# Unsplit weights and operands in a full float32 product: the mixers' output projections and the mixed output projection

## The chip, the cores and the metric

The kernel runs on one core of one Trainium2 chip. The metric is the device time of one execution in microseconds (us). TensorE (PE) multiplies, VectorE (DVE) and ScalarE (ACT) do elementwise work, GpSimd (POOL) issues the gathers and SyncE (SP) the loads of weights.

## The reference, cut to what matters

Two blocks run one after the other on 256 tokens of width 1024. The first has two layers of a hybrid mixer and a gated feed-forward part. The change lies in the two mixers:

```python
def hybrid_mixer(h, w_in, ret_out, ..., ssd_out, w_o):
    u = h @ w_in
    q, k, v, g_ret, z, xbc, dt, gate_ret, gate_ssd = split(u)
    yr = silu(g_ret) * rmsnorm(retention(rotary(q), rotary(k), v))     # 256 x 2048
    o_ret = yr @ ret_out                                               # 2048 -> 1024
    ys = rmsnorm_by_group(ssd(conv(xbc), dt) * silu(z)) * ssd_norm_w   # 256 x 2048
    o_ssd = ys @ ssd_out                                               # 2048 -> 1024
    merged = sigmoid(gate_ret) * o_ret + sigmoid(gate_ssd) * o_ssd
    return merged @ w_o                                                # 1024 -> 1024
```

`x = x + hybrid_mixer(rmsnorm(x))`, then the feed-forward part. The second block (attention, Fourier and pooling branches, and a layer of experts picked by keys) comes before and after: its work on the context runs first, and the gathering of its experts for the context goes on as background work under both mixers.

## The kernel before

Activations lie with features on the partitions: a tile is 128 features by 256 tokens, eight of them (NB) make the width. Weights come in units of 128 x 1024 float32 (512 KB): eight blocks of 128 x 128 for one column block of the output. `Stream` (class at line 232) works through a list of steps, one or two units each. It keeps four loads in flight (`stage`, four buffers, line 328, on SP's queue) and splits up to three units ahead (`split`, three buffers): `split_one` writes a high half in the rounded type fp32r on ACT (line 304) and the remainder, the low half, on DVE (line 305). A step marked `raw` gets the unit as it was loaded, without a split; the Fourier and pooling constants and the expert keys already run so.

A product of split weights and split operand is three matmuls (`mm3`, lines 448 to 450): high x high, high x low, low x high. `proj` does this for the eight blocks of a unit, `pairs` for a row of units, two units to one PSUM tile, with an `evac` that takes each pair out of PSUM. The operands are split too: `halves` (lines 455, 456, or 458, 459 with a scale) writes the high half on ACT and the low half on DVE. Two such operands exist, x2 and y2; layer 0 reads the residual from y2 and collects the mixers' outputs in x2, layer 1 the other way round.

In `mixer` the steps of a layer stand in this order, with 213 units in all: q and k of heads 0 to 2 and v and gate of heads 0 and 1; a flush; **ret0** (8 units: first half of ret_out); the other heads, z and x of group 0; **ret1** (8); groups 1 and 2; **ssd0** (8: first half of ssd_out); group 3 and the first gate; a flush; **ssd1** (8); the second gate (gs, 8); **wo** (8); then the feed-forward part. The operand of ret0 and ret1 comes from `finish` of each head (line 735, then halves), that of ssd0 and ssd1 from `six` of each group (line 882, then halves), that of wo from the evac of the second gate (line 915, then halves with scale). Chains of small steps (a head's scores and values, a group's scan) are set some steps after their projections (`later`), and lie between the matmuls of whatever runs then: group 0's chain in ret1, group 2's in ssd0.

The background (`peer_jobs`) is a list of jobs that each step releases by a credit: a slot of 1.75 steps gathers 1 MB of expert rows on POOL's queue, takes a dot product on DVE (line 1476) and adds the row to an accumulator on DVE (line 1487); jobs of routing sort keys on DVE. Each background instruction is held behind the latest split (`queue`, `st.last`). The order on each engine within these bounds is the scheduler's.

Of the kernel before, what the change touches and what calls it, by code (L numbers as in the profile page):

```python
# [10 lines left out]
F32 = mybir.dt.float32  # L11
F32R = mybir.dt.float32r
# [218 lines left out]

class Stream:
# [121 lines left out]
def tile_model(ctx: ExitStack, tc: tile.TileContext, a: dict, out: bass.AP):  # L354
# [28 lines left out]
    x2 = keep.tile([128, 2, NB, T], F32R, name="x2")  # L383
    y2 = keep.tile([128, 2, NB, T], F32R, name="y2")
    xh, xl, yh, yl = x2[:, 0], x2[:, 1], y2[:, 0], y2[:, 1]
# [185 lines left out]
    def pairs(arr, i0, n, evac, m=x2, kb=NB, k0=0, wide=False):  # L571
# [13 lines left out]
        for b in range(2 if wide else 0, n):  # L585
            def go(w, b=b):
                if b % 2 == 0:
                    held[0] = mm(2, T)
                proj(held[0][:, b % 2], w, m, k0, kb)
                if b % 2 or b == n - 1:  # L590
                    evac(b // 2, held[0])
            st.w(go, (arr, i0 + b), width=kb * 128)
# [16 lines left out]
    sides = ((y2, x2), (x2, y2))  # L609

    def mixer(l):
        W = a[f"first{l}"]
        o_ret, o_ssd = arena(ORET, NB, T), arena(OSSD, NB, T)
        x2, y2 = sides[l]
        xh, xl, yh, yl = x2[:, 0], x2[:, 1], y2[:, 0], y2[:, 1]
# [73 lines left out]
        def head_vg(h):  # L689
# [42 lines left out]
            def finish():  # L732
                p = stat(T)
                spread(y[1], p)
                V.scalar_tensor_tensor(fin, fin, 0.5, bc(p[:, None, :], [128, 4, T]), op0=OP.mult, op1=OP.mult)
                b = 4 * (h % 2)
                halves(yh[:, b:b + 4], yl[:, b:b + 4], fin)
# [12 lines left out]
        def ret_half(kh, i0):  # L750
# [6 lines left out]
            pairs(W, i0, 8, evac, y2)  # L757
# [18 lines left out]
        def group_x(g, i0):  # L776
# [101 lines left out]
            def six():  # L878
                p = stat(T)
                spread(y[1], p)  # L880
                for b in range(4):
# [18 lines left out]
        def ssd_half(kh, i0):  # L900
# [6 lines left out]
            pairs(W, i0, 8, evac, y2)  # L907

        def gate_ssd(i0):
            def evac(i, p):  # L910
# [5 lines left out]
                halves(yh[:, s], yl[:, s], t, 0.5)  # L916
# [16 lines left out]
        head_qk(0)  # L933
        st.w(dt_step, (W, FIRST_AT["dt"]), width=256)
# [592 lines left out]
    def peer_dense(l, filler=None, rate=0.0, between=None, middle=None):  # L1527
# [7 lines left out]
        wh, wl = [[w[:, i] for i in range(3)] for w in (yh, yl)]  # L1535
# [83 lines left out]
        def prep(i):  # L1619
# [4 lines left out]
            halves(wh[i % 3], wl[i % 3], f)  # L1624
# [194 lines left out]
```

## Time and profile before

| what | value |
|---|---|
| time, median of 3 runs | 4349.99 us (4347.65 to 4356.72) |
| the profiled execution: time, span | 4350.16 us, 4348.4 us |
| PE busy, matmul records | 4016.6 us (92%), 31186 |
| DVE busy | 3483.3 us (80%) |
| ACT busy | 2206.7 us (51%) |
| mean granted clock of PE | 0.964 |
| splits on DVE (line 305) | 1243, 1500.8 us |
| the two mixers without feed-forward | 344 to 982 us and 1204 to 1763 us of the span |

PE's busy share counts pipelined records that overlap, so 92% is not 92% of what PE can do; the distance between starts tells more. Shares over the whole span hide the stages: DVE is busy 90% or more in most of the slices from 430 to 2000 us, where the mixers and the background run together.

### The profile page before, as it was taken

To read this page: it belongs to the slowest core of one execution; us is meant where nothing else is said; L and a number is where in the kernel's file an instruction comes from. 1 tells how busy PE (TensorE), PEld (TensorE's weight loads), DVE (VectorE), ACT (ScalarE), POOL (GpSimd) and SP (SyncE) were. 2 spreads that over 40 slices of the span, in tenths; PEclk is the share of its full clock that TensorE was granted. 3 is DMA by queue.
4 is the path that set the end of the run, shared out by engine and by line. 5 is a ranking of instruction groups with operands and counts; after the bars stand their busy time and mean duration, and the time that the engine had idled before them with its cause. 6 is when DMAs were issued, how large, how long until landed. Compare 5 with 4: busy or idle time off the path is not lost.

```text
span 4348.4 us, 78619 instructions
## 1 busy us (share of the span) xinstructions
PE 4016.6 (92%) x31186; PEld 3804.5 (87%) x31186; DVE 3483.3 (80%) x6710; ACT 2206.7 (51%) x3473; POOL 393.0 (9%) x260
## 2 busy tenths in 40 slices
PE   8998888899999888998988899999999989899999
PEld 6887877789999888997878889999988988899999
DVE  5678999999989999998899986665575799855555
ACT  5655545554545555445744445555445444444444
POOL 0001111122222112221100000000000000000000
PEclk9998999999999999999999999999999999999999
DMA  6666765688878777886764588776644445776665
GB/s 210 213 209 239 251 234 202 249 321 317 315 286 335 257 261 292 315 331 234 257 219 155 170 281 258 241 239 215 186 139 135 152 144 179 260 231 206 206 187 151
DMA packets 293314, 1008.77 MB, mean 232 GB/s; under 512 B 25745, under 2 KB 92945, under 8 KB 255185
## 3 DMA queue, kind: packets, MB, share of 16 engines
q1 hardware_dynamic: 250608, 698.32, 49.5%
q0 software_dynamic: 36864, 268.45, 16.3%
q10 hardware_dynamic: 5472, 36.97, 2.1%
q8 instruction: 245, 4.01, 0.4%
q14 instruction: 125, 1.02, 0.1%
HBM read 966.94 MB, written 36.70 MB: 231 GB/s over the span
## 4 chain that ended last, share of the span: by engine, by line
PE 56%; DVE 33%; issue 5%; ACT 3%; DMA 3%; SPq 0%; DVEq 0%; ACTq 0%
PE mm L450 11%; PE mm L448 10%; PE mm L449 10%; DVE w L305 9%; PE ot L448 4%; PE ot L450 4%; PE ot L449 4%; DVE rows L1476 3%; DVE acc L1487 3%; DVE arena L1566 2%; ACT w L304 2%; PE st L449 1%; PE st L450 1%; PE st L448 1%; DMA rows<-gates 1%
## 5 line engine op out<-in xcount | busy, mean ns | idle before, releaser
L305 DVE TENSOR_TENSOR w<-stage,w 128x1024 fp32r<-128x1024 f32 (+1 forms) x1243 | 1500.8, 1213 | 571.8 <-ACT w L304 566.6
L304 ACT ACTIVATE w<-stage 128x1024 fp32r<-128x1024 f32 (+1 forms) x1243 | 1301.0, 1051 | 940.6 <-PE mm L450 474.7
L450 PE MATMUL mm<-x,w 128*128 128x256 f32 x4896 | 1402.4, 287 | 64.9 <-DVE w L305 64.2
L448 PE MATMUL mm<-x,w 128*128 128x256 f32 x4896 | 1409.8, 288 | 37.5 <-ACT x L458 10.8
L449 PE MATMUL mm<-x,w 128*128 128x256 f32 x4896 | 1398.0, 286 | 2.8 <-DVE x L459 1.8
L450 PEld LDWEIGHTS mm<-x,w 128*128 128x128 f32 x4896 | 940.3, 192 | 82.4 <-DVE w L305 79.7
L448 PEld LDWEIGHTS mm<-x,w 128*128 128x128 f32 x4896 | 942.5, 193 | 57.4 <-ACT w L304 13.7
L449 PEld LDWEIGHTS mm<-x,w 128*128 128x128 f32 x4896 | 941.5, 193 | 11.6 <-issue 5.0
L450 PE MATMUL mm<-y,w 128*128 128x256 f32 x1776 | 517.6, 293 | 47.8 <-DVE w L305 47.0
L1470 POOL DMA_INDIRECT rows<-in_table,idx x256 | 392.8, 1534 | 1843.0 <-DVE acc L1487 1219.5
L448 PE MATMUL mm<-y,w 128*128 128x256 f32 x1776 | 520.3, 293 | 28.1 <-ACT w L304 12.3
L449 PE MATMUL mm<-y,w 128*128 128x256 f32 x1776 | 512.7, 289 | 1.6 <-DVE y L456 0.9
L450 PE MATMUL ot<-y,w 128*128 128x256 f32 (+1 forms) x1616 | 454.7, 282 | 3.3 <-DVE w L305 3.3
L448 PE MATMUL ot<-y,w 128*128 128x256 f32 (+1 forms) x1616 | 454.7, 282 | 1.5 <-DVE arena L1131 1.5
L449 PE MATMUL ot<-y,w 128*128 128x256 f32 (+1 forms) x1616 | 454.1, 281 | 1.2 <-DVE y L456 1.2
L450 PEld LDWEIGHTS mm<-y,w 128*128 128x128 f32 x1776 | 347.7, 196 | 59.3 <-DVE w L305 57.8
L448 PEld LDWEIGHTS mm<-y,w 128*128 128x128 f32 x1776 | 349.0, 197 | 35.5 <-ACT w L304 14.4
L449 PEld LDWEIGHTS mm<-y,w 128*128 128x128 f32 x1776 | 348.8, 197 | 5.2 <-issue 2.9
L1487 DVE SCALAR_TENSOR_TENSOR acc<-rows,dots,acc 128x1024 f32<-128x1024 f32 x254 | 324.2, 1276 | 0.0
L1476 DVE SCALAR_TENSOR_TENSOR rows<-rows,h 128x1024 f32<-128x1024 f32 x256 | 311.1, 1215 | 7.3 <-DMA rows<-in_table,idx 7.2
L448 PEld LDWEIGHTS ot<-y,w 128*128 128x128 f32 (+1 forms) x1616 | 302.1, 187 | 6.8 <-DVE arena L1131 2.2
L450 PEld LDWEIGHTS ot<-y,w 128*128 128x128 f32 (+1 forms) x1616 | 302.5, 187 | 4.6 <-DVE w L305 4.5
(354 smaller groups left out, 5514.1 us busy)
## 6 DMA issues: line engine op xcount, KB each, us to landing
stage<-in_dense SPq DMA_DIRECT2D x512, 512.0 KB, 4.0
stage<-in_first SPq DMA_DIRECT2D x392, 512.0 KB, 5.5
stage<-in_mix SPq DMA_DIRECT2D x151, 512.0 KB, 4.3
stage<-in_mod SPq DMA_DIRECT2D x96, 512.0 KB, 4.6
gates<-rows ACTq DMA_DIRECT2D x32, 1024.0 KB, 4.5
rows<-gates SPq DMA_DIRECT2D x32, 1024.0 KB, 8.3
stage<-in_peer SPq DMA_DIRECT2D x50, 512.0 KB, 3.9
stage<-in_first SPq DMA_DIRECT2D x32, 448.0 KB, 5.6
```

Of the source, the lines that this page charges most:

```text
L304: nc.scalar.activation(h[:, :width], w, AF.Copy)
L305: self.last = nc.vector.tensor_sub(l[:, :width], w, h[:, :width].bitcast(F32))
L448: PE.matmul(o, sh, m[:, 0], start=start, stop=False, skip_group_check=True)
L449: PE.matmul(o, sh, m[:, 1], start=False, stop=False, skip_group_check=True)
L450: PE.matmul(o, sl, m[:, 0], start=False, stop=stop, skip_group_check=True)
L1470: G.indirect_dma_start(out=b, out_offset=None, in_=table, in_offset=bass.IndirectOffsetOnAxis(ap=idx[:, tt, s:s + 1], axis=0))
L1476: queue(V.scalar_tensor_tensor(buf[i][:, :D], buf[i][:, :D], 1.0, h2[:, tt], op0=OP.mult, op1=OP.mult, accum_out=d), st.last)
L1487: queue(V.scalar_tensor_tensor(acc[:, tt], up, d, acc[:, tt], op0=OP.mult, op1=OP.add), st.last)
L1566: V.tensor_scalar(x[:, 0, j], iota, xt[:, 0, t + j:t + j + 1], xt[:, 2, t + j:t + j + 1], op0=OP.is_equal, op1=OP.mult)
```

## The change

The units of ret0, ret1, ssd0, ssd1 and wo in both layers become `raw`: no split of their 80 units, and one matmul of float32 weights and float32 operand for each block in place of three. Their operand is written once, in float32, where both halves were written before: by DVE at the end of `finish` and `six`, by ACT at the second gate. For that the place of an operand is taken anew as a float32 tile of half the size (`take`, `View`): from after the first head's q and k to after wo. All else in the mixers, and everything outside them, keeps its form.

```diff
+    def take(side, dtype=F32R):
+        if dtype is F32R:
+            place[side] = operands.tile([128, 2, NB, T], F32R, name=side, tag=side)
+        else:
+            place[side] = operands.tile([128, NB, T], F32, name=side + "f", tag=side)
...
-    def pairs(arr, i0, n, evac, m=x2, kb=NB, k0=0, wide=False):
+    def pairs(arr, i0, n, evac, m=x2, kb=NB, k0=0, wide=False, raw=False):
...
-                proj(held[0][:, b % 2], w, m, k0, kb)
+                if raw:
+                    for k in range(kb):
+                        PE.matmul(held[0][:, b % 2], w[:, k * 128:k * 128 + 128], m[:, k0 + k], start=k == 0,
+                                  stop=k == kb - 1, skip_group_check=True)
+                else:
+                    proj(held[0][:, b % 2], w, m, k0, kb)
...
-            st.w(go, (arr, i0 + b), width=kb * 128)
+            st.w(go, (arr, i0 + b), width=kb * 128, raw=raw)
...
+        yside = sides[l][1]
+        yf = View(lambda: place[yside])
...
-                V.scalar_tensor_tensor(fin, fin, 0.5, bc(p[:, None, :], [128, 4, T]), op0=OP.mult, op1=OP.mult)
                 b = 4 * (h % 2)
-                halves(yh[:, b:b + 4], yl[:, b:b + 4], fin)
+                V.scalar_tensor_tensor(yf[:, b:b + 4], fin, 0.5, bc(p[:, None, :], [128, 4, T]), op0=OP.mult, op1=OP.mult)
...
-            pairs(W, i0, 8, evac, y2)
+            pairs(W, i0, 8, evac, yf, raw=True)
...
-                    V.scalar_tensor_tensor(yg[:, b], yg[:, b], P("ssd_norm_w", l * 16 + 4 * g + b), p,
+                    V.scalar_tensor_tensor(yf[:, o + b], yg[:, b], P("ssd_norm_w", l * 16 + 4 * g + b), p,
                                            op0=OP.mult, op1=OP.mult)
-                o = 4 * (g % 2)
-                halves(yh[:, o:o + 4], yl[:, o:o + 4], yg)
...
-                halves(yh[:, s], yl[:, s], t, 0.5)
+                S.activation(yf[:, s], t, AF.Copy, scale=0.5)
...
         head_qk(0)
+        st.f(lambda: take(yside, F32))
...
-        pairs(W, i["wo"], 8, lambda i, p: out_evac(i, p, P("norm_ffn_w", l * NB, NB)), y2)
+        pairs(W, i["wo"], 8, lambda i, p: out_evac(i, p, P("norm_ffn_w", l * NB, NB)), yf, raw=True)
         st.bg_rate(0, FFN_RATE)
+        st.f(lambda: take(yside))
```

DVE's queue at the start of ret0 in layer 0, before. x_82 is the operand, w_4637 and w_4667 are the first two units of ret0; L1476 and L1487 are a background slot, L678 to L680 a rotary step.

```order
L735 SCALAR_TENSOR_TENSOR arena<-arena,st 128x1024
L1446 TENSOR_REDUCE scratch<-scratch 128x16
L1476 SCALAR_TENSOR_TENSOR rows_88,dots<-rows_88,h_89 128x1024
L1448 SCALAR_TENSOR_TENSOR idx<-scratch 128x16
L456 TENSOR_TENSOR x_82<-arena,x_82 128x1024
L1487 SCALAR_TENSOR_TENSOR acc<-rows_87,dots,acc 128x1024
L305 TENSOR_TENSOR w_4637<-stage,w_4637 128x1024
L305 TENSOR_TENSOR w_4667<-stage,w_4667 128x1024
L678 TENSOR_TENSOR arena<-mm,cst 128x512
```

The same place now (L735 has become L767, L1476 and L1487 are L1507 and L1518, the rotary step L709 to L711):

```order
L767 SCALAR_TENSOR_TENSOR x2f<-arena,st 128x1024
L1477 TENSOR_REDUCE scratch<-scratch 128x16
L1507 SCALAR_TENSOR_TENSOR rows_91,dots<-rows_91,h_92 128x1024
L1479 SCALAR_TENSOR_TENSOR idx<-scratch 128x16
L1518 SCALAR_TENSOR_TENSOR acc<-rows_90,dots,acc 128x1024
L709 TENSOR_TENSOR arena<-mm,cst 128x512
L710 SCALAR_TENSOR_TENSOR arena<-mm,cst 128x256
L711 TENSOR_TENSOR arena<-mm,cst 128x256
L1507 SCALAR_TENSOR_TENSOR rows_88,dots<-rows_88,h_92 128x1024
```

The operand is complete with its first instruction, and the low half and the two splits are gone from behind it.

SP's queue of weight loads around ret0 in layer 0, before, with what each load waits for:

```order
L328 DMA stage<-in_first 128x1024 [waits DMAHW2_49,DVE_49,Activation_49]
L328 DMA stage<-in_first 128x1024 [waits DMAHW3_49,DVE_49,Activation_49]
L328 DMA stage<-in_first 128x1024 [waits DMAHW4_49,DVE_49,Activation_49]
L328 DMA stage<-in_first 128x1024 [waits DMAHW5_49,DVE_49]
L328 DMA stage<-in_first 128x1024 [waits DMAHW6_49,DVE_49]
L328 DMA stage<-in_first 128x1024 [waits DMAHW7_49,DVE_49]
```

The same loads now:

```order
L338 DMA stage<-in_first 128x1024 [waits DMAHW2_49,PE_49]
L338 DMA stage<-in_first 128x1024 [waits DMAHW3_49,PE_49]
L338 DMA stage<-in_first 128x1024 [waits DMAHW4_49,PE_49]
L338 DMA stage<-in_first 128x1024 [waits DMAHW5_49,PE_49]
L338 DMA stage<-in_first 128x1024 [waits DMAHW6_49,PE_49]
L338 DMA stage<-in_first 128x1024 [waits DMAHW7_49,PE_49]
```

The loads kept their place; each one's buffer is now freed by matmuls of a unit of ret0 and no longer by that unit's split.

## Rows read from the trace of the kernel before

**Rows 1.** Windows, layer 0: length, busy PE, PEld, DVE, ACT, POOL, clock, DMA, GB/s

```profile
490.50:514.00 23.50, 23.50 (x184) 23.42 (x184) 23.40 (x54) 13.51 (x23) 5.55 (x4) 0.92 0.89 330
514.00:643.00 129.00, 108.51 (x822) 104.21 (x821) 128.38 (x334) 63.86 (x102) 17.68 (x14) 0.93 0.70 247
643.00:686.00 43.00, 35.05 (x252) 30.97 (x252) 41.82 (x89) 22.45 (x32) 7.96 (x4) 0.94 0.52 178
686.00:784.00 98.00, 79.42 (x584) 74.04 (x584) 93.19 (x183) 54.15 (x83) 14.08 (x11) 0.92 0.66 231
784.00:819.00 35.00, 32.32 (x244) 29.15 (x244) 31.91 (x45) 22.50 (x34) 5.97 (x4) 0.95 0.68 252
...
903.00:927.00 24.00, 23.62 (x186) 23.62 (x187) 20.84 (x26) 10.04 (x16) 7.00 (x5) 0.93 0.85 308
927.00:954.00 27.00, 24.81 (x205) 24.18 (x203) 26.75 (x35) 14.46 (x26) 6.49 (x5) 1.00 0.94 359
954.00:982.00 28.00, 23.51 (x192) 22.90 (x192) 27.10 (x36) 15.35 (x29) 7.12 (x5) 1.00 0.88 326
sum 638.00, PE 541.50 PEld 515.64 DVE 611.80 ACT 334.55 POOL 106.92; mean PE 54.15 PEld 51.56 DVE 61.18 ACT 33.46 POOL 10.69
```

**Rows 2.** The same view, layer 1, a leading and a changed stage together

```profile
1204.00:1334.00 130.00, 121.18 (x924) 118.89 (x923) 114.74 (x188) 65.16 (x108) 31.13 (x20) 0.92 0.76 286
1334.00:1476.00 142.00, 134.82 (x1087) 129.84 (x1085) 134.51 (x192) 80.08 (x125) 32.78 (x22) 0.99 0.84 313
1476.00:1599.00 123.00, 106.89 (x803) 99.19 (x804) 116.96 (x186) 70.05 (x108) 20.20 (x16) 0.93 0.68 251
...
sum 559.00, PE 507.51 PEld 485.99 DVE 522.05 ACT 306.70 POOL 119.31; mean PE 101.50 PEld 97.20 DVE 104.41 ACT 61.34 POOL 23.86
```

**Rows 3.** Waits of PE: total, times, longest; three of 344:982, one of 1204:1763

```profile
PE mm L450 <- DVE w L305: 48.2, 30, 6.4
PE mm L449 <- DVE w L305: 13.5, 7, 5.0
PE mm L448 <- ACT w L304: 13.0, 8, 3.6
...
PE mm L450 <- DVE w L305: 26.2, 17, 4.0
```

**Rows 4.** Timeline of PE: start, duration, line; first and last matmul of one unit

```profile
1265.26 0.28 PE L448 MATMUL mm<-w,x 128*128 128x256 f32 x1
...
1267.94 0.28 PE L450 MATMUL mm<-w,x 128*128 128x256 f32 x1
```

**Rows 5.** Line 1172, full float32 products: one run in the timeline, all records

```profile
3274.27 2.86 PE L1172 MATMUL mm<-stage,arena 128*128 128x256 f32 x12
L1172 PE MATMUL mm<-stage,arena x48: 379/379/484, 91.7 to 3276.7; 128*128 128x256 f32 x48
```

**Rows 6.** Groups by line and shape: count, busy us, mean ns, idle before

```profile
L305 DVE TENSOR_TENSOR w<-stage,w 128x1024 fp32r<-128x1024 f32 x1199 | 1456.0, 1220 | 561.6 <-ACT w L304 556.5 <-PE mm L450 2.5 <-PE st L492 0.9
L304 ACT ACTIVATE w<-stage 128x1024 fp32r<-128x1024 f32 x1199 | 1261.5, 1056 | 903.1 <-PE mm L450 438.2 <-PE st L450 355.9 <-DMA stage<-in_first 24.3
L459 DVE SCALAR_TENSOR_TENSOR x<-arena,x 128x512 fp32r<-128x512 f32 x16 | 10.8, 683 | 0.7 <-ACT x L458 0.7
```

**Rows 7.** Timeline of DVE at the start of ret0, layer 0

```profile
481.90 1.21 DVE L735 SCALAR_TENSOR_TENSOR arena<-arena,st 128x1024 f32<-128x1024 f32 x1
...
484.59 1.21 DVE L456 TENSOR_TENSOR x<-arena,x 128x1024 fp32r<-128x1024 f32 x1
...
486.92 2.35 DVE L305 TENSOR_TENSOR w<-stage,w 128x1024 fp32r<-128x1024 f32 x2
```

**Rows 8.** Timeline of PE there

```profile
488.19 0.58 PE L450 MATMUL mm<-x,w 128*128 128x256 f32 x1 [6.42 <-DVE w L305]
```

**Rows 9.** Issues of weight loads: count, KB, us to landing; 490:514, then 927:982

```profile
stage<-in_first SPq DMA_DIRECT2D x6, 512.0 KB, 5.0
...
stage<-in_first SPq DMA_DIRECT2D x17, 512.0 KB, 7.0
```

More of the change, by code (lines that the diff above doesn't have):

```diff
@@ L229, in bc, with __init__, __getitem__ @@
     return ap.to_broadcast(shape)
+class View:
+    def __init__(self, now):
+        self.now = now
+    def __getitem__(self, k):
+        return self.now()[k]
 class Stream:
@@ L381, in tile_model, with parts @@
     res = keep.tile([128, NB, T], F32, name="res")
-    x2 = keep.tile([128, 2, NB, T], F32R, name="x2")
-    y2 = keep.tile([128, 2, NB, T], F32R, name="y2")
-    xh, xl, yh, yl = x2[:, 0], x2[:, 1], y2[:, 0], y2[:, 1]
+    operands = ctx.enter_context(tc.tile_pool(name="operands", bufs=1))
+    place = {}
+    def take(side, dtype=F32R):
[3 more added lines that the diff above has]
+            place[side] = operands.tile([128, NB, T], F32, name=side + "f", tag=side)
+    take("x2")
+    take("y2")
+    def parts(side):
+        return [View(lambda: place[side])] + [View(lambda i=i: place[side][:, i]) for i in range(2)]
+    x2, xh, xl = parts("x2")
+    y2, yh, yl = parts("y2")
     AR = keep.tile([128, N_ARENA], F32, name="arena")
@@ L607, in tile_model @@
     TQ, ORET, OSSD = 9728, 10240, 12288
-    sides = ((y2, x2), (x2, y2))
+    sides = (("y2", "x2"), ("x2", "y2"))
     def mixer(l):
@@ L613, in mixer @@
         o_ret, o_ssd = arena(ORET, NB, T), arena(OSSD, NB, T)
-        x2, y2 = sides[l]
-        xh, xl, yh, yl = x2[:, 0], x2[:, 1], y2[:, 0], y2[:, 1]
+        yside = sides[l][1]
+        (x2, xh, xl), (y2, yh, yl) = [parts(side) for side in sides[l]]
+        yf = View(lambda: place[yside])
         row = arena(8576, T)
@@ L880, in six @@
                 spread(y[1], p)
+                o = 4 * (g % 2)
                 for b in range(4):
-                    V.scalar_tensor_tensor(yg[:, b], yg[:, b], P("ssd_norm_w", l * 16 + 4 * g + b), p,
+                    V.scalar_tensor_tensor(yf[:, o + b], yg[:, b], P("ssd_norm_w", l * 16 + 4 * g + b), p,
                                            op0=OP.mult, op1=OP.mult)
-                o = 4 * (g % 2)
-                halves(yh[:, o:o + 4], yl[:, o:o + 4], yg)
             def chain():
@@ L906, in evac @@
                     V.tensor_add(o, o, p)
-            pairs(W, i0, 8, evac, y2)
+            pairs(W, i0, 8, evac, yf, raw=True)
         def gate_ssd(i0):
@@ L1534, in peer_dense @@
         hot = [shaped(w[:, 1024 * i:], (2, 4, 128)) for w in (AR, AR[:, 10240:]) for i in range(2)]
-        wh, wl = [[w[:, i] for i in range(3)] for w in (yh, yl)]
         slots = [w[:, o:o + 256] for w in (AR[:, 2048:8192], flat(h2), flat(acc), rowbuf[3], AR[:, 12288:])
@@ L1623, in prep @@
             V.tensor_mul(w, w, held[i // 8][:, :, i % 8, :])
-            halves(wh[i % 3], wl[i % 3], f)
+            halves(yh[:, i % 3], yl[:, i % 3], f)
         def up(i):
```

## The prediction

> **What bounds the kernel now.** I read the windows over the two mixers first, because the change touches nothing outside them; then who TensorE (PE) waits for there; then the price of one product in each form; last the order of VectorE (DVE) and of the weight loads around one changed stage. Both feed-forward parts and all that follows stand in the same order before and after, so everything outside the mixers is costed at nothing.
>
> In the mixer of layer 0, DVE is busy 611.8 of 638 us, PE's records 541.5 [rows 1]. The stage that leads up to ret1, 514 to 643, has DVE busy 128.38 of 129, and ret1 itself, 643 to 686, has 41.82 of 43 [rows 1]. DVE is the bound there. In layer 1 the two are nearer: DVE 522 of 559, PE records 507.5 [rows 2]. What PE waits for is the splitting of weights: 48.2 us in layer 0 and 26.2 in layer 1 by the line that waits longest [rows 3]. So the kernel is bound by DVE in layer 0 and by both in layer 1, and the change takes from DVE and gives to PE.
>
> **What one product costs.** Before, a block of 128 weights is multiplied by three matmuls. Their starts are 117 ns apart: 23 steps between 1265.26 and 1267.94 [rows 4]. The record's 280 ns is a pipelined duration and not the price. A block is thus 0.350 us, a unit of eight blocks 2.80 us. The full float32 product stands in the trace too, in the Fourier step of line 1172: twelve records of the same shape take 2.86 us with 0.38 for the last, so 11 steps, 226 ns each [rows 5]. The code issues 8 such products a call in 3 calls, 24 in all, and the row has 48: one product is two records, 0.451 us. A unit becomes 3.61 us, 0.81 more. There are 40 such units in a layer (8 in each of ret0, ret1, ssd0, ssd1, wo), 80 in all: PE gets 65 us more.
>
> The Trainium skill's page Perfetto Trace Analysis, section Engine Utilization (the note under its table), gives the array half its output rate for the form FP32_LOW_HIGH; by that rule a product would take 0.226 us, and PE would lose 80 us where the trace has it gain 65. The count of 48 records for 24 products speaks against the rule here.
>
> **What is removed.** Each of the 80 units loses its split: 1.220 us on DVE and 1.056 us on ScalarE (ACT) [rows 6]. That is 97.6 and 84.5 us. The operand's low half goes as well: 16 times 1.21 us on DVE (line 456, at 484.59 [rows 7]) and 8 times 0.683 us at the second gate [rows 6]. DVE loses 122.5 us in all, about 61 a layer, ACT about 100. Neither sum is a gain by itself. For one changed stage of 8 units it is 9.8 us off DVE and 6.5 on PE, so each pair of stages has to be gone through.
>
> *The operand's new place* costs nothing: it may be written when the old tile's last reader, the first head's q and k, is done, and its first write, in the first `finish`, comes some 15 units (42 us) later; without that cover the write would wait for one unit.
>
> *Layer 0, 344 to 514.* The operand of ret0 is ready at 483.1, the end of the 1.21 us at 481.90 [rows 7]. Before, its low half follows at 484.59 and the first weights' low half at 486.92, and PE resumes at 488.19 after 6.42 us of waiting [rows 7, 8]. From 483.1 to 514 is 30.9 us. After, nothing stands between the operand and PE, and 64 products take 28.9: a gain of 2.0. An earlier low half is 1.2 more. On the other side a load now waits for PE: a stage buffer is freed by the unit's last matmul, not by its split. The third split after the stage needs the buffer of the seventh unit, which ends 3.6 us before the stage does. With 5.0 us for the transfer [rows 9], 1.06 and 1.22 for the split, it is done 3.7 us after the end of the stage; before, it waited for the buffer of split weights, freed at that end, and was done 2.3 after. DVE thus loses 1 to 2 us at the exit, up to 3.4 where the transfer takes 7.0 [rows 9]. PE has three units of 2.80 us in hand there, so it does not wait. Behind the waiting split on ACT stand the stage's last evac, which three PSUM tiles for pairs cover, and the background's small steps, for which DVE's next slot waits. Taken: -1.
>
> *514 to 686 (ret1).* Two low halves (2.4) and the first two units' splits (2.4) leave a stage in which DVE has no idle time: -4.8. In the changed stage DVE falls from 41.8 to about 34, and PE decides. The stage of ssd0 shows what PE does beside the products: 35.0 us less 22.4 for the products is 12.6, the state-space chain and its waits. So 28.9 + 12.6 = 41.5 against 43: -1.5. Together -6; the ends are -12.2 (all of DVE's relief) and 0.
>
> *686 to 819 (ssd0).* The leading stage gives the same -4.8. The changed stage is nearer to PE's limit: 41.5 against 35, +6.5. A unit that needs no split can start while DVE is still at the convolution, which I take at the time of one unit, 3: together about -1; the ends are -12.2 and +6.5.
>
> *819 to 927 (ssd1).* Two low halves, the ACT half of 1.05 in front of the start, and two or three splits make -6. The stage itself is already at PE's pace (24 us for 22.4 of products), so it grows by 4.9 to 6.5: 0.
>
> *927 to 982 (second gate, wo).* In the gate DVE loses 2.7 and two splits, but PE's records fill 24.81 of 27 us and the DMA engines 0.94 of their time [rows 1]: -2 at most. wo goes from 28.0 to 28.9 plus about 1 for its start: +2. Sum 0.
>
> Layer 0: -1 -6 -1 +0 +0 = -8.
>
> *Layer 1.* DVE has slack ahead of ret0 (114.74 of 130 [rows 2]), so the first pair pays PE's +5, gets back 2.3 because the operand's halves are gone from the start of the stage, and pays 1 at the exit: +3 (ends -2, +6). The second has PE's records at 134.82 and DVE at 134.51 of 142: -3 (ends -9, +4). The third is like its sibling in layer 0, -1; the fourth -1; the fifth 0. Layer 1: -2.
>
> **Sum.** -10 us against the profiled execution's own 4350.16 us (its span is 4348.4, and 1.8 lies around it), which is within 0.2 us of the median 4349.99: **4340 us**.
>
> **Where the order was needed.** The order of DVE shows that at ret0 only the background's work is left behind the operand, and that the first split of the following stage comes after several of its slots; the order of the loads shows the six loads that now wait for PE. No other queue is moved past anything that matters: POOL's order is the same, and SP's differs in the mixers alone.
>
> **Rivals.**
>
> *A: DVE's relief passes through.* If the products of ret1 and ssd0 run early, under the convolutions that DVE is late with, PE's longer units are hidden. For it: 74.7 us of PE's waiting in layer 0 is for splits [rows 3]. Against: the chain's matmuls stand between the products on PE's queue, in order. Then the second and third pair of layer 0 and the third of layer 1 give about 10 each instead of 6, 1 and 1, -30 in place of -8: -32, **4318 us**.
>
> *B: PE becomes the bound in all ten stages, slower than before.* It decides if PE arrives at a changed stage no earlier than now, so that no head start exists. Then ret0, ssd1 and wo pay 5.5 each in both layers (+33), ssd0 6.5 and 8.5, ret1 -1.5 and -0.5 (+13). The leading stages give back low halves (about 11), first splits (about 10) and the gate (4). 46 - 25 = +21: **4371 us**. For it: layer 1's PE records already fill 134.82 of 142. Against: DVE's 128.38 of 129.
>
> *C: a full product costs one record.* If one record of 226 ns were the whole product, a unit would be 1.80 us instead of 2.80, and PE would lose 80 us beside DVE's 122.5; the background's transfers (DMA engines at 0.85 to 0.94 [rows 1]) then leave about half of DVE's relief: -60, **4290 us**. Against: the 48 records of rows 5.
>
> That the change does not do what it says is no rival: the order has runs of products with the undivided operand and weights, 64 to each changed stage.
>
> **How the numbers follow.** Forecast 0.44, with its own range 4330 to 4352; A 0.30; B 0.22; C 0.04. About 0.2% (8.7 us) is what a measurement of this kernel can tell from no change, so faster means under 4341.3 and slower over 4358.7. The forecast's middle lies on the first bound: 0.20 of its 0.44 fall below and 0.24 inside. With A (0.29 below, 0.01 inside) and C that makes 0.53 faster, 0.25 same; B's 0.22 is slower. The range takes A's lower part and B's centre: 4308 to 4372, and leaves out C, A's tail and the far half of B.
>
> **What would show it right or wrong.** In the profile after: 1280 records for the full products of the mixers' outputs, 226 ns apart in an unbroken run; 1163 splits in place of 1243; PE's wait of 6.4 us ahead of ret0 gone or under 3; ret0, ssd1 and wo at 29 to 31 us in both layers, ret1 near 41, ssd0 at 36 to 42; the stages ahead of ret1 and ssd0 4 to 6 us shorter in layer 0; the third load behind a changed stage issued after a matmul, with DVE idle for 1 to 3 us at the exit. The forecast fails by its price if the records are not 226 ns apart, by its cover if the leading stages are no shorter (then B), or if ret1 and ssd0 get shorter by 10 (then A). DVE idle over 5 us at each exit would be a cost that I have too low.

## The result, and the profile after

The changed kernel takes **4311.2 us** (median of 4 runs, 4305.5 to 4318.3) where the kernel before takes 4353.4 beside it: ratio 0.990, 95% interval 0.9885 to 0.9914. It is faster by 37 to 50 us. The forecast was 4340, the range 4308 to 4372: the time lies in the range, at its lower end. The profiled execution after is the longest of its four (4318.3, span 4316.5), and that of before one of the shorter ones (4350.2, span 4348.4), so the traces differ by 32 us only, the medians by 42.

The page of the profile after: span, busy time of each engine, and one group of its fifth part (the splits on DVE).

```profile
span 4316.5 us, 77045 instructions
PE 4028.0 (93%) x30546; PEld 3784.7 (88%) x30546; DVE 3375.7 (78%) x6606; ACT 2107.0 (49%) x3375; POOL 383.0 (9%) x260
...
L315 DVE TENSOR_TENSOR w<-stage,w 128x1024 fp32r<-128x1024 f32 (+1 forms) x1163 | 1406.3, 1214 | 590.9 <-ACT w L314 588.1
```

80 splits are gone, as forecast, and 640 records fewer are on PE: 1920 out, 1280 in. (Line 315 is 305 of before, 314 is 304, 471 to 473 are 448 to 450; the new product is line 615.)

Windows of layer 0 after, stage by stage: up to ret0, ret0, up to ret1, ret1, up to ssd0, ssd0, all of ssd1, the second gate, wo (columns: length, busy PE, PEld, DVE, ACT, POOL, clock, DMA share, GB/s). Their lengths can't be set against those of [rows 1], whose edges lie up to 7 us beside PE's products: the last product of ret1 ended at 681.3 there, not at 686, and the first of ssd0 began at 776.7, not at 784. The table further down goes by the products.

```profile
344.00:471.30 127.30, 108.90 (x765) 105.34 (x763) 119.18 (x369) 60.26 (x93) 16.25 (x11) 0.88 0.58 205
471.30:496.00 24.70, 24.53 (x114) 21.36 (x114) 20.83 (x59) 6.65 (x16) 4.49 (x4) 1.00 0.78 297
496.00:619.00 123.00, 108.34 (x813) 105.21 (x814) 118.09 (x306) 58.41 (x95) 20.25 (x14) 0.93 0.71 257
619.00:657.00 38.00, 36.16 (x193) 29.53 (x192) 35.90 (x96) 18.62 (x31) 3.95 (x4) 1.00 0.62 221
657.00:757.00 100.00, 82.79 (x588) 76.93 (x587) 94.09 (x186) 50.41 (x80) 16.30 (x12) 0.88 0.62 223
757.00:791.00 34.00, 33.94 (x184) 27.91 (x183) 27.43 (x42) 19.81 (x31) 5.23 (x4) 1.00 0.75 275
791.00:897.60 106.60, 97.62 (x655) 88.05 (x654) 87.47 (x140) 47.66 (x78) 20.39 (x15) 0.95 0.75 278
897.60:920.70 23.10, 22.48 (x193) 22.28 (x192) 22.68 (x29) 11.88 (x22) 6.51 (x5) 1.00 0.95 343
920.70:949.00 28.30, 28.23 (x133) 24.57 (x133) 17.26 (x27) 9.29 (x21) 6.39 (x5) 1.00 0.86 321
```

DVE still fills most of the stage ahead of ret1 (118.09 of 123); in ret1 itself PE's records now fill as much as DVE (36.16 and 35.90 of 38), and in ssd0 PE is busy throughout. The same view of layer 1, one window for each pair of a leading and a changed stage, the last for the gate and wo; it answers to [rows 2].

```profile
1174.50:1304.60 130.10, 123.16 (x854) 118.01 (x852) 101.65 (x177) 53.83 (x95) 29.34 (x20) 0.93 0.77 293
1304.60:1441.70 137.10, 135.37 (x1007) 127.56 (x1006) 122.80 (x182) 66.02 (x112) 29.77 (x21) 1.00 0.83 311
1441.70:1566.20 124.50, 114.71 (x771) 103.72 (x770) 109.73 (x180) 64.79 (x104) 19.50 (x16) 0.93 0.71 258
1566.20:1676.40 110.20, 98.85 (x655) 90.52 (x654) 89.22 (x142) 46.48 (x79) 22.58 (x15) 0.94 0.70 257
1676.40:1733.20 56.80, 53.09 (x322) 47.97 (x322) 42.49 (x56) 20.12 (x43) 13.58 (x9) 0.97 0.89 330
```

DVE now has 14 to 28 us of slack in each window, PE 1.7 to 11: the bound has moved towards PE here. What PE waits for, in the windows 344:950 and 1175:1740 (total us, times, longest), against [rows 3]:

```profile
PE mm L473 <- DVE w L315: 30.3, 20, 4.8
PE mm L472 <- DVE w L315: 15.1, 9, 3.8
PE mm L471 <- ACT w L314: 7.3, 3, 3.7
...
PE mm L473 <- DVE w L315: 13.3, 12, 2.7
PE st L509 <- DVE arena L903: 5.5, 2, 3.6
```

In layer 0 its waits for splits fell from 74.7 to 52.7 us, in layer 1 the longest line from 26.2 to 13.3.

**Where the time went.** The best ruler is the end of PE's last product of each changed stage (an evac can be late by itself). The table is worked out from the traces of before, of after and of every experiment below: the distance between such ends, the first from the first rotary step of the layer; "rest" is the span without the two sums.

```
                    layer 0                                layer 1
            ret0  ret1  ssd0  ssd1   wo    sum    ret0  ret1  ssd0  ssd1   wo    sum    rest
before     160.7 167.5 138.1 106.8  51.1  624.2  117.6 138.3 127.7 108.1  51.4  543.1  3181
e1_control 157.9 168.3 140.0 109.0  52.2  627.4  117.0 139.4 127.9 108.2  53.5  546.0  3183
e2_layout  160.5 167.6 137.9 106.3  51.9  624.2  118.3 137.3 129.1 108.4  53.4  546.5  3161
after      153.3 161.2 134.1 106.6  51.3  606.5  118.3 137.1 124.5 110.1  56.8  546.9  3163
f1_after   153.2 160.1 132.7 104.1  52.3  602.6  118.2 137.0 124.2 110.4  54.0  543.8  3172
e3_layer0  153.2 158.5 135.6 104.6  51.1  603.1  118.5 136.8 124.3 109.7  52.2  541.6  3171
e4_layer1  160.6 167.7 137.8 106.3  51.9  624.4  118.0 138.0 116.8 106.6  55.7  535.1  3159
f2_at64    151.4 162.6 134.1 104.6  52.0  604.7  119.2 138.2 120.7 107.5  56.7  542.2  3191
f3_at128   160.6 167.6 138.0 107.1  51.2  624.5  117.8 139.0 124.7 107.0  51.2  539.7  3194
f4_w128    153.3 161.3 135.3 105.1  51.7  606.7  118.9 137.9 122.0 110.2  53.0  541.9  3189
g1_kept    153.3 164.4 137.1 107.2  54.2  616.2  118.5 139.3 124.5 107.3  57.4  547.0  3170
g2_six     145.3 159.0 130.2 104.4  52.3  591.2  115.7 132.2 116.1 112.8  47.7  524.4  3179
g3_five    153.3 154.0 135.2  97.3  55.6  595.4  118.4 135.4 119.1 100.4  56.7  530.0  3140
g4_chains  157.6 156.5 133.7 107.0  53.3  608.1  118.4 136.4 118.4 106.8  51.5  531.5  3169
```

So the change takes 18 to 22 us out of layer 0's mixer, **nothing out of layer 1's**, and 9 to 20 out of stages in which it changes no instruction.

Each row is one execution. Between two executions of one program (before and e1_control, after and f1_after) a mixer differs by up to 4 us, a stage by up to 3, and the rest by up to 9. Three traces are of an execution well under the median of its kernel: e2_layout (4333.4 us, median 4341.1), e4_layer1 (4320.2, median 4334.8) and g3 (4267.5, median 4276.2). What is only a few us in the table is read with that in mind.

### The profile page after: what moved, and what is told of

It is laid out like the page before. It is cut to its first block, busy times and chain, and to the rows that moved or that the text cites. A ratio compares the mean times of both kernels' runs of the same rounds, so it can differ in the third digit from the quotient of the medians.

```text
span 4316.5 us, 77045 instructions
## 1 busy us (share of the span) xinstructions
PE 4028.0 (93%) x30546; PEld 3784.7 (88%) x30546; DVE 3375.7 (78%) x6606; ACT 2107.0 (49%) x3375; POOL 383.0 (9%) x260
## 4 chain that ended last, share of the span: by engine, by line
PE 58%; DVE 29%; DMA 5%; issue 5%; ACT 3%; POOL 0%; SPq 0%; DVEq 0%; ACTq 0%; POOLq 0%
PE mm L473 10%; PE mm L471 10%; PE mm L472 10%; DVE w L315 8%; PE ot L471 4%; PE ot L473 4%; PE ot L472 4%; PE mm L615 4%; DVE acc L1518 3%; DVE rows L1507 3%; DVE arena L1596 2%; DMA stage<-in_first 2%; ACT w L314 2%; DMA rows<-gates 1%; PE st L471 1%
## 5 line engine op out<-in xcount | busy, mean ns | idle before, releaser
L315 DVE TENSOR_TENSOR w<-stage,w 128x1024 fp32r<-128x1024 f32 (+1 forms) x1163 | 1406.3, 1214 | 590.9 <-ACT w L314 588.1
L314 ACT ACTIVATE w<-stage 128x1024 fp32r<-128x1024 f32 (+1 forms) x1163 | 1216.0, 1050 | 912.5 <-PE mm L473 353.4
L473 PE MATMUL mm<-x,w 128*128 128x256 f32 x4576 | 1301.6, 285 | 49.3 <-DVE w L315 49.0
L471 PE MATMUL mm<-x,w 128*128 128x256 f32 x4576 | 1311.5, 287 | 18.7 <-ACT x L481 9.0
L472 PE MATMUL mm<-x,w 128*128 128x256 f32 x4576 | 1297.8, 284 | 1.2 <-DVE x L482 1.1
L473 PEld LDWEIGHTS mm<-x,w 128*128 128x128 f32 x4576 | 876.7, 192 | 63.5 <-DVE w L315 61.1
L471 PEld LDWEIGHTS mm<-x,w 128*128 128x128 f32 x4576 | 878.7, 192 | 36.1 <-ACT x L481 9.6
L472 PEld LDWEIGHTS mm<-x,w 128*128 128x128 f32 x4576 | 877.6, 192 | 9.1 <-issue 4.3
L1501 POOL DMA_INDIRECT rows<-in_table,idx x256 | 382.8, 1495 | 1825.7 <-DVE acc L1518 1221.4
L473 PE MATMUL mm<-y,w 128*128 128x256 f32 x1456 | 420.1, 290 | 35.4 <-DVE w L315 35.2
L471 PE MATMUL mm<-y,w 128*128 128x256 f32 x1456 | 421.7, 290 | 19.5 <-ACT w L314 10.6
L472 PE MATMUL mm<-y,w 128*128 128x256 f32 x1456 | 415.0, 286 | 0.0
L1518 DVE SCALAR_TENSOR_TENSOR acc<-rows,dots,acc 128x1024 f32<-128x1024 f32 x254 | 324.7, 1278 | 0.4
L473 PEld LDWEIGHTS mm<-y,w 128*128 128x128 f32 x1456 | 282.3, 195 | 46.0 <-DVE w L315 44.9
L1507 DVE SCALAR_TENSOR_TENSOR rows<-rows,h 128x1024 f32<-128x1024 f32 x256 | 311.6, 1217 | 11.9 <-DMA rows<-in_table,idx 11.9
L471 PEld LDWEIGHTS ot<-y,w 128*128 128x128 f32 (+1 forms) x1616 | 302.0, 187 | 7.4 <-DVE arena L1162 2.2
L473 PEld LDWEIGHTS ot<-y,w 128*128 128x128 f32 (+1 forms) x1616 | 302.2, 187 | 7.0 <-DVE w L315 6.8
L471 PEld LDWEIGHTS mm<-y,w 128*128 128x128 f32 x1456 | 283.3, 195 | 24.6 <-ACT w L314 12.7
L472 PEld LDWEIGHTS ot<-y,w 128*128 128x128 f32 (+1 forms) x1616 | 302.2, 187 | 2.6 <-DVE y L479 1.5
```

The lines of the kernel that those rows point to most:

```text
L314: nc.scalar.activation(h[:, :width], w, AF.Copy)
L315: self.last = nc.vector.tensor_sub(l[:, :width], w, h[:, :width].bitcast(F32))
L471: PE.matmul(o, sh, m[:, 0], start=start, stop=False, skip_group_check=True)
L472: PE.matmul(o, sh, m[:, 1], start=False, stop=False, skip_group_check=True)
L473: PE.matmul(o, sl, m[:, 0], start=False, stop=stop, skip_group_check=True)
L1501: G.indirect_dma_start(out=b, out_offset=None, in_=table, in_offset=bass.IndirectOffsetOnAxis(ap=idx[:, tt, s:s + 1], axis=0))
```

## The experiments

Ratios are to the kernel before, run in the same comparison, with 95% intervals. The changed kernel ran beside f2 to f4 (as f1), not beside the e and g runs; these are set against its ratio of 0.990.

**The same kernel, the layout alone, each layer alone.** `RAWS` lists the changed stages of each layer. `e1_control` is the kernel before; `e2_layout` takes the operands' tiles from their own pool, as the change does, and changes no product:

```diff
+RAWS = ((), ())                                                    # e2_layout
+RAWS = (('ret0', 'ret1', 'ssd0', 'ssd1', 'wo'), ())                # e3_layer0
+RAWS = ((), ('ret0', 'ret1', 'ssd0', 'ssd1', 'wo'))                # e4_layer1
...
-            pairs(W, i0, 8, evac, yf, raw=True)
+            pairs(W, i0, 8, evac, yf if f"ret{kh}" in RAW else y2, raw=f"ret{kh}" in RAW)
```

> The kernel before, unchanged, as a second trace of it. The trace of after is 10.6 us ahead of the trace of before at its first rotary step (342.4 against 353.0 us), ahead of anything that the change touches. Theory R (executions differ there): ratio 1.000 within 0.001, and the first rotary step of this trace is several us away from 353.0. Theory S (the change moved something ahead of the mixers): this trace has it within 2 us of 353.0.

Measured: 1.0001 (0.9989 to 1.0014). The first rotary step of this trace stands at 346.8 us, 6 us from 353.0, so executions differ there, as theory R has it; the changed kernel's second trace has it at 348.3. One mixer differs by up to 3 us between these two executions (table).

> Only the operands' tiles come from a pool of their own, as in the change, and are taken anew in front of each of the five stages; all products, splits and halves as before. Theory S (the gain at the start is one of memory places): 6 to 12 us faster than before, first rotary step near 343 us. Theory R and the forecast: no difference, within 4 us.

Measured: 4341.1 against 4358.4, **0.9970** (0.9959 to 0.9981), with every instruction of every engine in the order of before. The 17 us are more than either theory expected, and the first rotary step is at 347.4, as in e1_control: the gain is not at the start. The mixers are as before (624.2 and 546.5); 20 us in the traces are in the rest. I had put everything outside the mixers at nothing. In the last dense stage PE never stops, so the count of records in a stretch of 320 us is its pace. The window 3860:4180 of the kernel before, then of e2_layout, then of the changed kernel:

```profile
3860.00:4180.00 320.00, 320.00 (x2707) 320.00 (x2706) 181.06 (x225) 151.54 (x225) 0.00 (x0) 1.00 0.68 206
```

```profile
3860.00:4180.00 320.00, 320.00 (x2745) 320.00 (x2744) 183.10 (x229) 154.60 (x229) 0.00 (x0) 1.00 0.69 205
```

```profile
3860.00:4180.00 320.00, 320.00 (x2719) 320.00 (x2719) 181.31 (x227) 152.70 (x227) 0.00 (x0) 1.00 0.65 203
```

320 us over the count is 118.2, 116.6 and 117.7 ns from one split matmul to the next, all at the full clock. The same code runs at three paces. A pace belongs to a program and not to an execution: e1_control has 2706 records in this window where before has 2707, and f1_after has 2719 as after.

> The five stages are changed in layer 0 alone. Forecast's sum for layer 0: 8 us faster. Relief theory (DVE's relief passes through wherever DVE is late, rival A): 18 us or more faster, since the traces have layer 0's mixer 17.9 us shorter.

Measured: 0.9908 (0.9893 to 0.9924), 4315.8 us. Layer 0's mixer is 21 us shorter than before (603.1), as the relief theory has it and not the forecast.

> The five stages are changed in layer 1 alone. Forecast's sum for layer 1: 2 us faster. Relief theory: nothing, 0 within 3 us, since the traces have the part from layer 1's first step to its last unchanged in length. Layout or other theories that put a gain outside of the mixers: 8 us or more.

Measured: 0.9948 (0.9933 to 0.9962), 4334.8 us. The gain outside of the mixers is there (rest 3159 in place of 3181), as the layout theory has it; against the layout run, layer 0 alone is worth 25 us by the medians and layer 1 alone 6; both together, 0.990, are no better than layer 0 alone within the intervals. In the trace of e4 layer 1's mixer is 11 us shorter than e2_layout's, in that of after it isn't; but this one execution of e4 was 15 us shorter than its kernel's median. Most of the difference is ssd0: 116.8 against 124.5. The place to look is its start. The timelines of ACT (the first split behind ret1) and of PE (its next work) in the changed kernel, and three windows of 6 us there:

```profile
1438.74 1.06 ACT L314 ACTIVATE w<-stage 128x1024 fp32r<-128x1024 f32 x1 [4.27 <-DMA stage<-in_first]
...
1446.93 1.86 PE L509 MATMUL st<-cst,arena 128*128 128x1 f32 x8 [3.57 <-DVE arena L903]
```

```profile
1440.00:1446.00 6.00, 3.37 (x23) 2.96 (x21) 6.00 (x7) 3.78 (x5) 0.59 (x1) 1.00 0.64 227
1446.00:1452.00 6.00, 5.07 (x23) 5.07 (x24) 4.11 (x9) 0.82 (x1) 1.42 (x2) 0.50 0.79 298
1452.00:1458.00 6.00, 6.00 (x49) 6.00 (x49) 4.69 (x10) 2.48 (x6) 0.61 (x1) 0.93 0.73 261
```

The same two views of e4_layer1:

```profile
1461.42 1.06 ACT L316 ACTIVATE w<-stage 128x1024 fp32r<-128x1024 f32 x1 [3.03 <-DMA stage<-in_first]
...
1469.60 1.05 PE L511 MATMUL st<-cst,arena 128*128 128x1 f32 x8 [2.31 <-DVE arena L915]
```

```profile
1464.00:1470.00 6.00, 3.69 (x26) 3.30 (x24) 6.00 (x8) 2.46 (x4) 1.67 (x1) 1.00 0.78 264
1470.00:1476.00 6.00, 6.00 (x52) 6.00 (x53) 5.45 (x12) 2.63 (x5) 1.75 (x1) 1.00 0.82 274
1476.00:1482.00 6.00, 6.00 (x54) 6.00 (x53) 5.84 (x15) 3.48 (x7) 0.74 (x1) 1.00 0.87 337
```

Behind a changed stage the first splits wait for loads. Where ACT waited 4.27 us, DVE's work came late, PE stood still for 3.57 us, and it came back at half clock: 0.50 for the next 6 us, 23 records where e4 has 52. Where ACT waited 3.03 and PE 2.31, the clock stayed at 1.00. How long this pair (from ret1's last product to ssd0's) takes goes with its mean clock. Five executions in which both stages are changed, with four buffers and no split of their units, by length (e4, g4, f2, f4, f1), and last the kernel before:

```profile
1465.70:1582.50 116.80, 107.86 (x770) 96.81 (x769) 109.40 (x180) 64.03 (x103) 20.30 (x16) 1.00 0.76 273
1449.10:1567.50 118.40, 109.46 (x770) 98.45 (x769) 108.61 (x178) 63.84 (x102) 19.51 (x16) 0.99 0.76 269
1446.40:1567.10 120.70, 111.31 (x771) 100.37 (x770) 109.49 (x180) 64.56 (x104) 19.54 (x16) 0.97 0.74 266
1452.30:1574.30 122.00, 112.69 (x771) 101.73 (x770) 109.14 (x180) 64.30 (x104) 19.50 (x16) 0.96 0.73 263
1444.20:1568.30 124.10, 114.71 (x770) 103.81 (x769) 109.01 (x180) 64.08 (x104) 19.54 (x16) 0.93 0.72 259
1471.70:1599.40 127.70, 110.60 (x835) 102.69 (x834) 121.66 (x191) 74.01 (x113) 21.81 (x16) 0.93 0.68 249
```

So the 8 us between e4 and after go with the clock of the execution. The kernel before loses as much to it here (0.93): the dips are not something that the change brought to this pair, and at an equal clock the changed pair is 3 us shorter. What decides how many dips an execution has is open; that the load which came 1.2 us later brought the one shown is argued from one pair of traces.

**The operands' place.** If the layout's gain were the operands' place against a boundary of 128 bytes, pads of 64 bytes should undo it or give it.

```diff
+    operands.tile([128, 16], F32, name="pad0", tag="pad0")         # f2_after_at64, ahead of the operands
...
+    keep.tile([128, 16], F32, name="pad0")                         # f3_before_at128, ahead of the operands
+    keep.tile([128, 16], F32, name="pad1")                         # and behind them
...
+    operands.tile([128, 24], F32, name="pad1", tag="pad1")         # f4_after_w128, ahead of the operands
+    keep.tile([128, 8], F32, name="pad0")                          # and ahead of the staged weights
```

> The changed kernel once more, for comparison on one chip with the three runs beside it. Expected by every theory: ratio to the kernel before 0.990, within 0.9885 to 0.9915, that is 40 to 50 us shorter.

Measured: 0.990 (0.9881 to 0.9919), 4312.6 us, as expected by every theory.

> The changed kernel with one unused tile of 64 bytes a partition ahead of the two operand tiles, so that both begin 64 bytes past a multiple of 128, as they did in the kernel before; nothing else moves. Place theory (the 17 us that the layout alone gave come from the operands' place against a 128-byte boundary): the split matmuls of the last dense stage go back from 117.8 to 118.3 ns apart, and the time rises by about 17 us over the changed kernel, ratio to before 0.994. Rival (another trait of the new layout gave them, such as which tile lies in which half of the memory): ratio 0.990 as without the pad, pace 117.8 or less. Rival (the layout gave nothing that repeats): 0.990 too, with the pace as it falls.

Measured: **0.9974** (0.9961 to 0.9986): 33 us slower than without the pad, twice what the theory gave. Both rivals are out.

> The kernel before with 64 unused bytes a partition ahead of the operand tiles and 64 behind them, so that both begin at a multiple of 128 bytes, while every later tile keeps its place against such a boundary; no instruction is another one. Place theory: as the layout run, ratio 0.997, within 0.995 to 0.9985, split matmuls of the last dense stage 116.7 to 117.8 ns apart. Both rivals: ratio 1.000, 118.3 ns apart.

Measured: 1.000 (0.9987 to 1.0013). The theory falls here: both tiles on multiples of 128, and no gain.

> The changed kernel with the staged weights and the split weights moved by 32 bytes, so that these too begin at a multiple of 128 (they began 96 bytes past one in the kernel before and after), the operands staying on a multiple. If the weights' place matters as the operands' does: the split matmuls come nearer than 116.7 ns and the ratio falls to 0.986. If only the operands' place matters: ratio 0.990, 116.7 to 117.8 ns.

Measured: 0.9948 (0.9931 to 0.9966): everything on multiples of 128, and 21 us slower than the changed kernel, against both expectations. The window 3860:4180 of f2, then of f3, then of f4:

```profile
3860.00:4180.00 320.00, 320.00 (x2669) 320.00 (x2668) 177.98 (x222) 150.03 (x223) 0.00 (x0) 1.00 0.65 200
```

```profile
3860.00:4180.00 320.00, 320.00 (x2669) 320.00 (x2668) 178.62 (x223) 150.03 (x224) 0.00 (x0) 1.00 0.68 203
```

```profile
3860.00:4180.00 320.00, 320.00 (x2699) 320.00 (x2698) 180.58 (x225) 151.24 (x224) 0.00 (x0) 1.00 0.66 202
```

119.9, 119.9 and 118.6 ns. What is shown: unused bytes alone move the pace, and in f2 and f4 the whole time by 33 and 21 us, most of it outside the mixers (rest 3191 and 3189, against 3163 and 3172). In f3 they moved the pace of this window as much as in f2 (118.2 to 119.9) and the whole time not at all, so the pace in this one window does not give the time. What is open: the rule. It isn't the 128-byte boundary, and the place alone doesn't settle it either: e2_layout and the changed kernel have equal places and 116.6 and 117.7. `g1_kept`, which like e2_layout splits all 1243 units, has 2745 records in this window too (116.6); e3, e4 and g4, which split fewer, have 2719 as the changed kernel. Why was not tried.

**What relieves and what costs.** `g1_kept` computes the splits of the 80 units all the same; `g2_six_blocks` leaves two of eight blocks out of each sum of the changed stages, so that its output isn't the reference's.

```diff
-                    if not req[i][2]:
+                    if req[i][2] in (False, "split"):              # g1_kept: split, and keep the whole too
...
-                    for k in range(kb):
+                    for k in range(kb - 2):                        # g2_six_blocks
```

> The changed kernel, but every weight block of the five changed stages is still split by ACT and DVE as before; the halves are computed into their buffer and no product reads them (the operands' halves are gone, as in the changed kernel). So TensorE has the dearer products and the other two engines have 80 splits of 1.05 and 1.22 us back. Theory (the gain is DVE's and ACT's relief from the weight splits, less what TensorE's products cost): the whole gain goes and part of TensorE's 53 us comes on top, ratio to before 1.000 to 1.010, that is 40 to 90 us above the changed kernel. Rival (the gain comes from the operands' halves no longer computed, or from the tiles' new places): ratio 0.990 to 0.993, no more than 15 us above the changed kernel.

Measured: 0.9955 (0.9938 to 0.9971), 4338.6 us: some 25 us above the changed kernel and about level with the layout alone. The weight splits' relief is worth about what the change gains beyond the layout. It is not the 40 to 90 us expected. In the table the splits cost 10 to 14 us in layer 0 (616.2) and 0 to 3 in layer 1 (547.0); that DVE, with its splits back, covers PE's dearer products again is the likely reason and not shown by itself. In layer 0 ret0 keeps its 7 us (153.3), which thus do not come from DVE's and ACT's time for the weight splits. Two things are left for them, and g1 does not part them: the operand's halves are no longer in front of the stage, and no product there waits for the split of its weights.

> The changed kernel, but the ten changed stages add up only the first six of the eight blocks of each sum; the products with the last two blocks are left out, all loads stay. A unit of weights then costs TensorE 6 x 0.434 = 2.60 us, about what it cost before the change (2.80), instead of 3.47: 80 x 0.87 = 69 us less. If TensorE sets the pace of the changed stages now: most of the 69 us shows, ratio 0.975 to 0.980. If DVE still sets it (the forecast's view of three stages of five): 10 to 30 us show, ratio 0.983 to 0.988. If neither does but the exits (loads that wait for their buffers): under 10 us, ratio 0.988 to 0.990.

Measured: 0.9833 (0.9814 to 0.9852), 4287.0 us, 26 to 29 us below the changed kernel, of 69 us taken from PE. That is the second case: DVE still sets much of the pace. By the table 11 to 15 us are in layer 0 and 19 to 22 in layer 1, of 35 each: layer 0 hides most of what PE does there, layer 1 a good third.

> The changed kernel with five buffers for staged weights instead of four, so that a load behind a changed stage can start one block earlier. Operands and split weights move by 4096 bytes. Exit theory (behind a changed stage the first splits wait for loads, TensorE runs dry for 3 to 6 us and, where the pause is long, comes back at half clock): 10 to 20 us shorter than the changed kernel, ratio 0.9855 to 0.988, and the granted clock in layer 1's group stages near 1.0. Rival (the exit's waits are covered or fall elsewhere): ratio 0.990, within 5 us of the changed kernel.

```diff
-    stage = ctx.enter_context(tc.tile_pool(name="stage", bufs=4))
+    stage = ctx.enter_context(tc.tile_pool(name="stage", bufs=5))
...
-    st = Stream(nc, stage, split, 4, 3)
+    st = Stream(nc, stage, split, 5, 3)
```

Measured: **0.9814** (0.9797 to 0.9831), 4276.2 us: some 36 us faster than the changed kernel, more than expected, and the fastest kernel of this study (the two traces differ by 51: that of after is its longest execution, this one its shortest). ACT's splits by shape, the idle time before them and what ended it, of the changed kernel and of this one:

```profile
L314 ACT ACTIVATE w<-stage 128x1024 fp32r<-128x1024 f32 x1119 | 1176.5, 1056 | 876.4 <-PE st L473 340.5 <-PE mm L473 319.7 <-DMA stage<-in_first 117.3
```

```profile
L314 ACT ACTIVATE w<-stage 128x1024 fp32r<-128x1024 f32 x1119 | 1175.1, 1055 | 777.6 <-PE st L473 359.4 <-PE mm L473 308.7 <-DMA stage<-in_first 58.5
```

Waits for loads were 24.3 us before [rows 6]; the change made 117.3 of them, a fifth buffer halves that. Its windows of layer 1's second to fourth pair have the clock at 1.00, 0.97 and 0.98:

```profile
1291.10:1426.50 135.40, 134.51 (x1007) 127.20 (x1006) 123.43 (x183) 67.71 (x113) 28.88 (x22) 1.00 0.89 334
1426.50:1545.60 119.10, 110.42 (x771) 99.85 (x770) 109.28 (x180) 64.51 (x103) 19.57 (x16) 0.97 0.73 266
1545.60:1646.00 100.40, 94.33 (x655) 86.13 (x654) 85.18 (x138) 45.57 (x76) 20.11 (x14) 0.98 0.76 271
```

Not all of it is the exits. The mixers gain 7 to 17 us each, but the rest gains 23 to 32; part of that is the pace, 116.6 ns in its last dense stage, and the buffer also moved the tiles. How much the fifth buffer would give the kernel before was not tried.

> Only the second retention projection and the first state-space projection of both layers are changed, with the layout of the changed kernel; the other three stages split as before. By the forecast's sum these two stages hold nearly all of the gain inside the mixers (7 of 10 us), and the first retention projection of layer 1 loses 7 us at its exit in the trace of the changed kernel, which is away here. If the stages add up: ratio 0.988 to 0.991, as good as the whole change or better. Rival (the gain is the relief summed over all stages, two fifths of it here): ratio 0.9935 to 0.9955.

```diff
+RAWS = (('ret1', 'ssd0'), ('ret1', 'ssd0'))
```

Measured: 0.9891 (0.9873 to 0.9909), 4311.1 us: two stages of five do as well as all. In layer 1 they take 12 to 15 us out of the mixer (531.5), where all five take nothing; in layer 0 the other three add 2 to 6. Of what all five lack in layer 1, 6 us are in ssd0, whose clock was 0.99 in this execution and 0.93 in those of the changed kernel, 3 in ssd1 and 3 to 5 in wo: these two seem to give back a part of the gain, by little more than two executions of one program differ. ret0 and its exit do not: the 7 us that the expectation puts there are not in the table (118.4 and 136.4, against 118.3 and 137.1).

## Why the prediction was right in its sign, and where it was off

**The price of a product.** Two records each, as forecast; they stand nearer than 226 ns. One run in ret0, where PE's wait of 6.42 us [rows 8] is now 1.03:

```profile
471.27 24.44 PE L615 MATMUL mm<-x2f,stage 128*128 128x256 f32 x112 [1.03 <-DVE x2f L767]
```

(24.44 - 0.38) / 111 = 217 ns, so a product is 0.434 us, a unit 3.47 and PE's addition 53 us instead of 65. The run of twelve in [rows 5] gave 226, a run of 112 gives 217: the price taken from the short one was too high. The rule of the Trainium skill's page Perfetto Trace Analysis, section Engine Utilization, that halves the output rate for FP32_LOW_HIGH is not borne out for a whole product: 640 products left 1280 records, and a product takes two of them, 0.434 us and not 0.226. The Trainium skill's page FP8 and Floating Point Precision, section TensorE Precision Notes, has true FP32 make four passes; here a product takes 434 ns, 3.7 times the 117 ns of one split matmul, which is near it.

**What was removed.** 80 splits, as counted. DVE's busy time fell by 107.6 us (122.5 forecast, from whole durations, which overlap), ACT's by 99.7 (100).

**Layer 0, stage by stage** (forecast, measured in the two traces of the changed kernel against before): ret0 -1, **-7.4 and -7.5**; ret1 -6, -6.3 and -7.4; ssd0 -1, -4.0 and -5.4; ssd1 0, -0.2 and -2.7; wo 0, +0.2 and +1.2. Sum -8 against -18 and -22. Against e1_control, the other trace of the kernel before, ret0 is -4.6 and the sum -21 and -25. The step that failed is ret0: I let 64 products stand behind the operand for 28.9 us, and it took 24.4 from 471.27 to 495.71. Sixteen of the 128 records had run ahead on the first half of the operand, 8 of them at 457.96, and the price was lower. One cause of the gain there I did not name: PE came back from its 6.42 us of waiting at the lower clock, and now it doesn't. The first 6 us, before and after:

```profile
488.00:494.00 6.00, 5.81 (x27) 5.81 (x28) 6.00 (x10) 1.21 (x3) 1.21 (x2) 0.50 0.79 287
```

```profile
471.30:477.30 6.00, 6.00 (x28) 5.30 (x29) 6.00 (x12) 1.25 (x5) 0.94 (x1) 1.00 0.44 113
```

At 118 ns the 27 split matmuls would have taken 3.2 us instead of 6, so by this estimate some 3 of the 7 us are the clock. ret1 was right in its sum, not in its parts: between PE's products the stage ahead went from 125.4 to 122.4 us (-3.0, forecast -4.8) and the stage itself from 42.2 to 38.8 (-3.4, forecast -1.5). In ssd0 both parts were wrong: the stage ahead did not shrink (95.4 to 96.8, at a clock of 0.88), and the stage itself, where I had the change pay 6.5, went from 42.6 to 37.3. The term that was wrong in both stages is what PE does beside the products, taken as a fixed 12.6 us from a window that began 7 us after the first product of ssd0. By the products it was 19.8 in ret1 and 20.2 in ssd0, and it fell to 11.0 and 9.5 (38.8 and 37.3 less 27.8 for 64 products): much of it had been waiting and slow clock (0.94 and 0.95 in these stages before [rows 1], 1.00 in both after).

**Layer 1**: +3, -3, -1, -1, 0, measured +0.7, -1.2, -3.2, +2.0, +5.4 (second trace +0.6, -1.3, -3.5, +2.3, +2.6). Sum -2 against +4 and +1. Here the forecast was close in its sum. In the traces of e4 and g4 layer 1 gains 8 to 15 us, of which 6 to 8 are an ssd0 at full clock; its dips, which the kernel before has as well, and the exits, which g3 shortens, decide what is seen.

**The exit** was costed at 1 to 2 us of DVE, with PE covered by three units in hand. The cause was right (a load waits for PE to free its buffer), the size not: 93 us more of ACT's waiting for loads in all, PE dry for 3.57 us behind ret1 of layer 1, and half a clock after it. In the 15 us behind a stage DVE waited under 2 us for ACT's splits at seven of ten exits, but 6.5 behind ret0 of layer 0 and 17.8 and 4.1 behind ret0 and ret1 of layer 1. That PE comes back slower from a pause stood nowhere in the sum; before the change it did so too (ahead of ret0 in layer 0, and in the pair of ssd0 in layer 1).

**Outside the mixers** I took zero because nothing moves in the order. The tiles moved in memory, and that gave 9 to 20 us of rest in the traces; e2_layout shows 17 us for it by the medians. The share in the changed kernel itself is not measured, and may be smaller: its last dense stage runs at 117.7 ns, that of e2_layout at 116.6.

**The rivals.** A gave 4318, nearest to the time, but 17 of the 42 us measured are the layout, which A does not have; without them the time would lie near 4328, between A and the forecast. That 4311 is so near to A is luck, and the range holds it, by 3 us, because A's time had been taken in. Its mechanism, products that run early and hide PE's price, is there in layer 0 (g2: 11 to 15 of 35 us show), in ret0 and ssd0 rather than in the second pair, and at less than the 10 us that A gave each. B, slower, is refuted as a whole; in layer 1 the bound did move towards PE. C is refuted by the records. The forecast was 29 us too high: 17 of them are the places of the tiles by e2_layout, some 10 are ret0 and ssd0 of layer 0. This is no closed sum: layer 1 came out 3 to 6 us worse than forecast, and 10 us of the medians' difference are not in the traces.

## What to carry to other kernels

Removing work from the busiest engine pays only in the stages that it bounds: two stages of five gave as much as all five. Where a buffer is now freed by a later engine, look at the first wait behind the stage, and try the change with one more buffer in the stream too (and the old kernel with it, which was not done here). Before a difference between two traces is explained, see how far two executions of one program differ in the same stage. And when tiles move in memory, run the new layout without the change first; otherwise its 17 us are credited to the wrong cause.

## What the hardware showed that I had not expected

The distance between back-to-back split matmuls of 256 columns, at the full clock, lies between 116.6 and 119.9 ns in the window 3860:4180 of all fourteen traces and is the same in two executions of one program; 64 unused bytes ahead of the operands took it from 117.7 to 119.9. The Trainium skill's page TensorE: Matmul & The Clock Gate, section Back-to-back issue gap, gives 262 cycles at 2.4 GHz for this size in isolation, 109 ns; with a weight load for each matmul no trace came below 116.6 in this window; the measurement decides. The granted clock went to the lower level (1.2 GHz, 0.50) after a pause of 3.57 us and stayed at the upper one after 2.31 us at the same place of the program; ahead of ret0 in layer 0 it was 0.50 after a pause of 6.42 us and 1.00 after 1.03.
